# SyncE's DMAs in program order, with q's high parts first and three things traced later

## The chip, the cores and the metric

The kernel runs on one core of a Trainium2 chip. The metric is the device time of one execution in microseconds (us). TensorE (PE) multiplies, VectorE (DVE) and ScalarE (ACT) work on the results, GpSimd (POOL) helps, and SyncE (SP) issues nearly all DMAs; ACT issues the rest.

## What is computed

One layer of a streaming encoder, in float32, for a prompt of 2048 rows of 1024 and a sample of 32 rows. The reference, cut to what matters here:

```
mod = c @ w_mod + b_mod;  shift, scale, gate = split(mod, 3)
h = rms_norm(x, g_pre) * (1 + scale) + shift
z = h @ w_in      # a, b, z_conv, q, k, v, z_attn, g_conv, g_attn
u = a * sigmoid(b)
y_conv = (silu(layer_norm(conv31(u) + dw_b)) * silu(z_conv)) @ w_conv_out
o = attention(q, k, v)    # 8 heads of 64, own chunk of 64 rows and the 8 chunks before
y_attn = (o * silu(z_attn)) @ w_attn_out
merged = sigmoid(g_conv) * y_conv + sigmoid(g_attn) * y_attn
y = x + gate * rms_norm(merged @ w_o, g_post)
```

The prompt starts with no history. The sample attends to 512 cached rows of k and v besides its own. The last 512 rows of k and v (the cached ones moved on, for the sample) and the last 30 rows of u are outputs too.

## The kernel before

Every product is made in three passes: an operand is split into a high part (rounded, made by ACT) and a low part (the difference, made by DVE or POOL), and high*high, high*low and low*high are added in PSUM. So each projection of 128 columns is 24 matmuls per segment of rows.

The prompt goes in four batches of 512 rows; the sample's 32 rows ride with the first (batch 0, whose segments are 272 columns wide). Each batch has these stages: V's projection; attention, with the other projections of the batch ("fill", in the order that `FILL(b)` lists) traced between its pieces; the gate columns and the two branches; the output projection with the next batch's GLU columns; the norm and the residual. In `FILL`, a letter is a group of columns (`q`, `k`, `a` and `b` for u, `z` for the attention gate, `c` for the conv gate, `m` for a piece of the modulation) and the digit its block.

Weights come as `raw` tiles (512 KB, two buffers), are split into `w` (1 MB, three buffers) and, where they are used again, kept in DRAM (`kept`, written by ACT's queue) and later read back into `w`. `weights()` is called at the start of each projection and loads four entries of the plan ahead, splits two ahead. A load must wait until its buffer is free.

Heads go in pairs, `hp` from 0 to 3. In batch 0, `q_proj(hp)` loads the pair's cached rows of v and k into `zcb` (256 KB each) and starts `cached_k`, whose four transposes `pk` on PE turn the cached k. The bias of a head lies skewed in DRAM: `bias_write(h)` writes `bias_d[h]` from `lrow_d` (384 KB, DRAM to DRAM), then two small masks (`msk`) over it, and `load_bias(h)` reads it into `bias` (two buffers); in batch 0 `load_bias(h)` first traces `bias_write(h + 2)`. `sink_q` makes `qh` (ACT) and `ql` (DVE) from a projection. `turn` makes the high and low parts of transposed scores, `pth` and `ptl`. `turn_o` transposes the sample's attention output (`po`). `spill_v` writes the batch's V rows to `vs_d` for the next batch.

What sets the order: the program is traced once by hand-written generators with a pace model (`pace.start(gen, delay)` traces a piece when the modelled PE time has moved on by the delay, in us). For the engines named in `ENGINES`, PE, DVE, ACT and POOL, the instructions stand as traced. SP is not among them: a scheduler places its DMAs, as early as buffers allow and stores late. On SP an issue waits on SyncE itself, and what stands behind it waits too.

```
LEAD, LEADU, LEADU0 = 0.36, -3.0, -1.0
ENGINES = {mybir.EngineType.PE, mybir.EngineType.DVE, mybir.EngineType.Activation, mybir.EngineType.Pool}
...
            if b < NB - 1:
                pace.start(spill_v(b, vcur), 100.0 if b == 0 else 30.0)
...
    ctx.enter_context(tc.manual_schedule(engines=ENGINES))
```

Of the kernel before, what the change touches and what calls it, by code (L numbers as in the profile page):

```python
# [11 lines left out]
AF = mybir.ActivationFunctionType  # L12
# [35 lines left out]
TP = (1, 1, 1)  # L48

LEAD, LEADU, LEADU0 = 0.36, -3.0, -1.0  # L50
ENGINES = {mybir.EngineType.PE, mybir.EngineType.DVE, mybir.EngineType.Activation, mybir.EngineType.Pool}


def FILL(b):

    part = dict(q=C_Q, k=C_K, a=C_A, b=C_B, z=C_ZA, c=C_ZC, m=C_MOD)
    order = "b0 a0 q1 k1 b1 m0 a1 m1 b2 m2 q2 m3 k2 m4 a2 m5 z0 m6 b3 m7 a3 z1 q3 k3 z2 z3 c0 c1 c2 c3" if b == 0 else \
        "q1 k1 z0 q2 k2 z1 q3 k3 z2 z3 c0 c1 c2 c3"
    return [(int(x[1]), part[x[0]]) for x in order.split()]


def dram(ap, off, dims):
    return bass.AP(tensor=ap.tensor, offset=ap.offset + off, ap=[list(d) for d in dims])
# [77 lines left out]
def mixer_kernel(ctx, tc, x_prompt, x_sample, c_prompt, c_sample, cache_conv, cache_k, cache_v,  # L141
# [3 lines left out]
    act = nc.scalar.activation  # L145
    G = nc.gpsimd
    pace = Pace()
# [345 lines left out]
    conv_ready, ln_done, gate_done = set(), {}, set()  # L493
# [78 lines left out]
    def mod_part(i):  # L572


        n, kp = i // 4, i % 4
        m4, bm, gr = aof[0:4, 3, 0:512], aof[0:2, 2, 0:512], aof[0:2, 1, 0:512]
        if kp == 0:
            nc.sync.dma_start(bm, dram(b_mod, 2 * D + n * 512, [[0, 2], [1, 512]]))
            nc.sync.dma_start(gr, dram(g_post, n * 512, [[0, 2], [1, 512]]))
        wh, wl = weights(("mod", 2 * kp, (4 + n) * 512))  # L580
        pm = pp_tile("pm")
        for kk in range(2):
            mm(pm[0:4], c4[:, 2 * kp + kk, :], wh[:, kk, :], kk == 0, False)
            mm(pm[0:4], c4[:, 2 * kp + kk, :], wl[:, kk, :], False, kk == 1)
            yield
        if kp == 0:
            act(m4, pm[0:4], AF.Copy)
        else:
            V.tensor_tensor(m4, pm[0:4], m4, op=OP.add)
        if kp == 3:  # L590
            pace.start(gate_row(n, m4, bm, gr), 4.0)
# [17 lines left out]
    def spill_v(b, vcur):  # L609
        for t in range(4):  # L610
            nc.sync.dma_start(vs_d[b][:, t], vcur[:, t].bitcast(F32))
            yield 6.0
# [20 lines left out]
    with tc.tile_pool(name="init", bufs=1) as ini:  # L633
        mraw, mparts, m4 = {}, {}, {}
# [177 lines left out]
    for b in range(NB):  # L812
# [5 lines left out]
        with tc.tile_pool(name="at", bufs=1) as at:  # L818
# [26 lines left out]
                    o = (nvs[0, 0, 512 - TS:512] if t == 4 else nvp[0, 0, t * P:(t + 1) * P])  # L845
                    nc.sync.dma_start(o.rearrange("t h d -> t (h d)"), vo[0:m, 0:512])
            if b < NB - 1:
                pace.start(spill_v(b, vcur), 100.0 if b == 0 else 30.0)


            qls.clear()
# [25 lines left out]
            def q_proj(hp):  # L877
                while hp > 1 and ("s", hp - 2) not in ready:
                    yield "wait"
                qk_alloc(hp)  # L880
                kk, _, qh, ql = att[hp]
                ck = None
                if b == 0:
                    ck = zcb[:, 2 * (hp % 2), 0:512].rearrange("p (t c) -> p t c", c=P)
                    cv = cvs[hp] = zcb[:, 2 * (hp % 2) + 1, 0:512].rearrange("p (t c) -> p t c", c=P)
                    nc.sync.dma_start(cv, cache_v[0, 0].rearrange("t h d -> t (h d)")
                                      [:, hp * P:(hp + 1) * P].rearrange("(t p) c -> p t c", p=P))
                    nc.sync.dma_start(ck, cache_k[0, 0].rearrange("t h d -> t (h d)")
                                      [:, hp * P:(hp + 1) * P].rearrange("(t p) c -> p t c", p=P))

                    pace.start(cached_k(hp, ck), 9.9 if hp == 0 else 3.0)

                def sink_q(o, c0, c1):
                    for s in range(2):
                        r = slice(64 * s, 64 * s + 64)
                        act(qh[r, s, c0:c1], o[r], AF.Copy, scale=-0.125)
                        act(qh[64 - 64 * s:128 - 64 * s, s, c0:c1], o[r], AF.Copy, scale=-0.125)
                        V.scalar_tensor_tensor(ql[r, s, c0:c1], o[r], -0.125, qh[r, s, c0:c1].bitcast(F32),
                                               op0=OP.mult, op1=OP.subtract)

                yield from proj(C_Q + hp * P, b, sink_q)
# [127 lines left out]
            class Unit:  # L1029
# [77 lines left out]
                def turn(self, c):  # L1107

                    if c == 0:
                        self.ph = at.tile([P, PTW], F32R, tag="pth", name="pth", bufs=2)  # L1110
                        self.pl = at.tile([P, PTW], F32R, tag="ptl", name="ptl", bufs=2)
                    if c >= len(self.chunks):
                        return
                    pt = ps.tile([P, 512], F32, tag="T", name="pt", bufs=2)
                    if self.g == 2:
                        sp = self.sp[0]
                        for j in range(4):
                            transpose(pt[:, j * TS:(j + 1) * TS], sp[0:TS, j * P:(j + 1) * P], ident[0:TS, 0:TS])
                        transpose(pt[0:TS, 4 * TS:5 * TS], sp[0:TS, 512:512 + TS], ident[0:TS, 0:TS])
                        jobs = [(P, 0, 0, 4 * TS), (TS, 4 * TS, 4 * TS, 5 * TS)]  # L1120
                    else:
                        q, part = self.chunks[c]
                        for jj, (i, j) in enumerate(part):
                            transpose(pt[:, jj * P:(jj + 1) * P], self.sp[i][:, j:j + P], ident)
                        jobs = [(P, 0, q * P, (q + len(part)) * P)]
                    for r, o, f0, f1 in jobs:
                        act(self.ph[0:r, f0:f1], pt[0:r, o:o + f1 - f0], AF.Copy)  # L1127
                        V.tensor_tensor(self.pl[0:r, f0:f1], pt[0:r, o:o + f1 - f0],
                                        self.ph[0:r, f0:f1].bitcast(F32), op=OP.subtract)

                def mix(self):
                    hp, s, g, f, nk = self.hp, self.s, self.g, self.f, self.nk
                    if g == 2:

                        pv = ps.tile([P, 512], F32, tag="PV", name="pvs")
                        for j in range(5):
                            k = P if j < 4 else TS
                            rt = att[hp][1][:, j, s, :] if j < 4 else vsam[hp // 2][0:TS, 2 * (hp % 2) + s, :]
                            for w, ptx in enumerate((self.ph, self.pl)):
                                mm(pv[0:TS, 0:P], ptx[0:k, j * TS:(j + 1) * TS], rt, j == 0 and w == 0, j == 4 and w == 1)  # L1140
                        th = at.tile([TS, HD], F32, tag="osh", name="osh", bufs=2)
                        if s == 0:
                            osm[hp] = at.tile([TS, P], F32, tag="osm", name="osm", bufs=2)
                        act(th, pv[0:TS, 0:HD], AF.Copy)
                        V.tensor_tensor(osm[hp][:, s * HD:(s + 1) * HD], pv[0:TS, HD:P], th, op=OP.add)
                        if s == 1:
                            pace.start(turn_o(hp), 1.0)
                    else:
                        e = [2 * g + 5, 2 * g + 6]
                        common = list(range(f[1], e[0]))  # L1150
                        jobs = [(kt, 0, 2) for kt in common]
                        jobs += [(kt, 0, 1) for kt in range(f[0], common[0])]
                        jobs += [(kt, 1, 1) for kt in range(common[-1] + 1, e[1])]
                        if g == 0:
                            pvt[s] = ps.tile([P, 512], F32, tag="PV", name="pv")
                        c0 = g * 256
                        for j, (kt, i, n) in enumerate(jobs):
                            for w, ptx in enumerate((self.ph, self.pl)):
                                off = i * nk[0] + (kt - f[i]) * P
                                rhs = view(ptx, off, [[nk[0] + (f[0] - f[1]) * P, 2], [1, P]] if n == 2 else [[1, P]])  # L1160
                                mm(pvt[s][:, c0 + i * P:c0 + (i + n) * P], vtile(hp, s, kt), rhs,
                                   j == 0 and w == 0, j == len(jobs) - 1 and w == 1)
                        if g == 1:
                            put_o(hp, s, pvt[s], 0, TB)
                    if s == 1 and g == (2 if b == 0 else 1):
                        ready.add(("o", hp))
                        gates()
# [287 lines left out]
```

## Time and profile before

| what | before |
|---|---|
| median of three runs | 1741.46 us (1741.26 to 1746.23) |
| the profiled execution's own time | 1743.5 us |
| its span, from first to last instruction | 1741.4 us |
| PE busy | 1674.9 us (96%) |
| DVE, ACT, POOL busy | 65%, 37%, 12% |
| mean granted TensorE clock | 0.991 of 2.4 GHz |
| moved by DMA | 361.27 MB, 207 GB/s |

The span is what the trace shows; 2.1 us of the execution's own time lie outside it. An engine that waits is idle in the profile, and the view of waits says for whom. SP is never busy by the profile; its rows show when each DMA was issued.

### The profile page before, as it was taken

To read this page: it belongs to the slowest core of one execution; us is meant where nothing else is said; L and a number is where in the kernel's file an instruction comes from. 1 tells how busy PE (TensorE), PEld (TensorE's weight loads), DVE (VectorE), ACT (ScalarE), POOL (GpSimd) and SP (SyncE) were. 2 spreads that over 40 slices of the span, in tenths; PEclk is the share of its full clock that TensorE was granted. 3 is DMA by queue.
4 is the path that set the end of the run, shared out by engine and by line. 5 is a ranking of instruction groups with operands and counts; after the bars stand their busy time and mean duration, and the time that the engine had idled before them with its cause. 6 is when DMAs were issued, how large, how long until landed. Compare 5 with 4: busy or idle time off the path is not lost.

```text
span 1741.4 us, 23645 instructions
## 1 busy us (share of the span) xinstructions
PE 1674.9 (96%) x9221; PEld 1425.8 (82%) x9221; DVE 1135.9 (65%) x2055; ACT 646.5 (37%) x1232; POOL 210.3 (12%) x171
## 2 busy tenths in 40 slices
PE   6988889999999999999999999999999999999997
PEld 4877789899877788888888888888888888888886
DVE  6568778796818767676745967773544967665423
ACT  6645444325611255523430055531330045531211
POOL 0224433003200000000220000001130000001120
PEclk9999899999999999999999999999999999999999
DMA  9775555733666764477655674365555674355553
GB/s 288 223 279 201 189 204 200 277 110 119 225 241 217 289 254 162 160 261 266 218 209 190 247 275 172 132 229 189 194 205 193 223 251 163 135 189 190 189 194 145
DMA packets 144870, 361.27 MB, mean 207 GB/s; under 512 B 9326, under 2 KB 89386, under 8 KB 116311
## 3 DMA queue, kind: packets, MB, share of 16 engines
q1 hardware_dynamic: 136119, 296.85, 49.7%
q10 hardware_dynamic: 8640, 62.92, 8.8%
q8 instruction: 73, 1.20, 0.3%
q14 instruction: 38, 0.31, 0.0%
HBM read 273.07 MB, written 91.77 MB: 210 GB/s over the span
## 4 chain that ended last, share of the span: by engine, by line
PE 63%; DMA 2%; DVE 1%; ACT 0%; POOL 0%; issue 0%; POOLq 0%; DVEq 0%; ACTq 0%; SPq 0%
PE pj L155 35%; PE py L155 8%; PE pv L155 4%; PE sps L155 3%; PE pt L159 3%; PE op L155 3%; PE oT L155 2%; PE oS L155 2%; PE vS L155 1%; PE vT L155 1%; PE oP L155 1%; DMA w<-kept 1%; DMA kept<-w 0%; PE pxt L159 0%; DMA raw<-in_w_in_dram 0%; DVE pre L136 0%
## 5 line engine op out<-in xcount | busy, mean ns | idle before, releaser
L155 PE MATMUL pj<-hh,w 128*128 128x512 f32 (+1 forms) x4800 | 975.8, 357 | 14.0 <-DVE aof L136 4.0
L155 PEld LDWEIGHTS pj<-hh,w 128*128 128x128 f32 x4800 | 782.1, 190 | 136.3 <-issue 7.9
L136 DVE SCALAR_TENSOR_TENSOR y<-u,dww,y 128x512 f32<-128x512 f32 (+1 forms) x480 | 348.2, 785 | 0.5
L1092 ACT ACTIVATE sp<-sp,mn 128x640 f32<-128x640 f32 (+5 forms) x136 | 103.7, 762 | 132.0 <-DVE mn L136 132.0
L1127 ACT ACTIVATE pth<-pt 128x256 fp32r<-128x256 f32 (+4 forms) x184 | 91.8, 500 | 130.1 <-PE pt L159 118.0
L234 ACT ACTIVATE w<-raw 128x1024 fp32r<-128x1024 f32 x86 | 90.3, 1053 | 99.2 <-DMA raw<-in_w_in_dram 30.5
L136 DVE TENSOR_TENSOR ptl<-pt,pth 128x256 fp32r<-128x256 f32 (+4 forms) x184 | 104.1, 566 | 24.3 <-ACT pth L1127 23.0
L136 DVE CUSTOM_DVE_ANT_0 sp<-sps,bias 128x640 f32<-128x640 f32 (+4 forms) x128 | 94.1, 736 | 23.2 <-PE sps L155 22.2
L155 PE MATMUL py<-ah,w 128*128 128x512 f32 (+1 forms) x480 | 95.7, 355 | 7.8 <-DVE t L136 5.7
L236 POOL TENSOR_TENSOR w<-raw,w 128x1024 fp32r<-128x1024 f32 x32 | 81.3, 2547 | 150.7 <-ACT w L234 114.2
L155 PEld LDWEIGHTS py<-ah,w 128*128 128x128 f32 x480 | 79.5, 191 | 21.3 <-DVE t L136 6.1
L136 DVE TENSOR_TENSOR w<-raw,w 128x1024 fp32r<-128x1024 f32 x54 | 69.5, 1288 | 41.5 <-ACT w L234 40.9
L159 PE MATMUL pt<-ident,sp 128*128 128x128 f32 (+1 forms) x600 | 94.4, 273 | 0.0
L155 PE MATMUL py<-cohi,w 128*128 128x512 f32 (+1 forms) x320 | 90.1, 357 | 1.5 <-DVE mg L136 1.5
L540 POOL TENSOR_TENSOR u<-y 128x512 f32<-128x512 f32 (+1 forms) x4 | 5.3, 1325 | 646.7 <-DVE y L136 593.8
L136 DVE TENSOR_SCALAR sp<-sp,ll 128x640 f32<-128x640 f32 (+5 forms) x136 | 78.6, 578 | 4.8
L155 PE MATMUL sps<-kk,qh 128*128 128x320 f32 (+1 forms) x224 | 69.8, 319 | 8.7 <-DVE mn L136 6.2
L159 PEld LDWEIGHTS pt<-ident,sp 128*128 128x128 f32 (+1 forms) x600 | 69.1, 140 | 3.6 <-issue 1.5
L155 PE MATMUL sps<-kk,ql 128*128 128x320 f32 (+1 forms) x224 | 68.1, 311 | 0.0
L1319 ACT ACTIVATE t<-pj 128x512 f32<-128x512 f32 (+1 forms) x40 | 20.7, 516 | 127.2 <-PE pj L155 127.2
L1355 POOL TENSOR_TENSOR mg<-mg,t 128x512 f32<-128x512 f32 (+1 forms) x32 | 46.4, 1449 | 155.6 <-issue 102.2
L155 PEld LDWEIGHTS py<-cohi,w 128*128 128x128 f32 x320 | 56.7, 188 | 9.8 <-DVE mg L136 2.2
(254 smaller groups left out, 2207.3 us busy)
## 6 DMA issues: line engine op xcount, KB each, us to landing
w<-kept SPq DMA_DIRECT2D x162, 1024.0 KB
kept<-w ACTq DMA_DIRECT2D x60, 1024.0 KB
raw<-in_w_in_dram SPq DMA_DIRECT2D x62, 512.0 KB
bias<-bias_d SPq DMA_DIRECT2D x32, 320.0 KB
xt<-in_x_prompt_dram SPq DMA_DIRECT2D x16, 512.0 KB
wm<-in_w_mod_dram SPq DMA_DIRECT2D x16, 512.0 KB
xr<-in_x_prompt_dram SPq DMA_DIRECT2D x16, 512.0 KB
vs_d<-vcur SPq DMA_DIRECT2D x12, 512.0 KB
```

Source lines behind the costliest of these rows:

```text
L136: return fn(out, *a, **k)
L155: nc.tensor.matmul(out, lhsT=lhsT, rhs=rhs, start=start, stop=stop)
L159: nc.tensor.transpose(out, in_, idn)
L234: act(wh, raw, AF.Copy)
L236: (V if on_v else G).tensor_tensor(wl, raw, wh.bitcast(F32), op=OP.subtract)
L540: G.tensor_tensor(s2[:, 0:YW], Y[2][:, 0:YW], Y[3][:, 0:YW], op=OP.add)
L1092: self.ex[i] = lambda: act(sp[0:m, 0:nk], sp[0:m, 0:nk], AF.Exp, bias=mn[0:m], scale=-1.0, accum_out=ll[0:m])
L1127: act(self.ph[0:r, f0:f1], pt[0:r, o:o + f1 - f0], AF.Copy)
L1319: pace.run(proj(C_GC + m * P, b, lambda o, c0, c1: act(t1[:, c0:c1], o, AF.Tanh, scale=0.5)))
L1355: G.tensor_tensor(mg, mg, t2, op=OP.add)
```

## The change

Five edits. SP joins the engines whose instructions stand in the order of the trace. In `sink_q` all four high parts are traced ahead of the two low parts, and in `turn` the high parts of all jobs ahead of the low ones. In `FILL` for batch 0 block 3 of q and k comes ahead of block 1 of z. `turn_o` is traced 3.0 later than its unit in place of 1.0. V's rows of batches 1 and 2 are written 100 later in place of 30. An assertion is added too, which makes no instruction.

```
-ENGINES = {mybir.EngineType.PE, mybir.EngineType.DVE, mybir.EngineType.Activation, mybir.EngineType.Pool}
+ENGINES = {mybir.EngineType.PE, mybir.EngineType.DVE, mybir.EngineType.Activation, mybir.EngineType.Pool,
+           mybir.EngineType.SP}
...
-    order = "b0 a0 q1 k1 b1 m0 a1 m1 b2 m2 q2 m3 k2 m4 a2 m5 z0 m6 b3 m7 a3 z1 q3 k3 z2 z3 c0 c1 c2 c3" if b == 0 else \
+    order = "b0 a0 q1 k1 b1 m0 a1 m1 b2 m2 q2 m3 k2 m4 a2 m5 z0 m6 b3 m7 a3 q3 k3 z1 z2 z3 c0 c1 c2 c3" if b == 0 else \
...
-                pace.start(spill_v(b, vcur), 100.0 if b == 0 else 30.0)
+                pace.start(spill_v(b, vcur), 100.0)
...
-                    for s in range(2):
-                        r = slice(64 * s, 64 * s + 64)
+                    rows = [slice(0, 64), slice(64, 128)]
+                    for s, r in enumerate(rows):
                         act(qh[r, s, c0:c1], o[r], AF.Copy, scale=-0.125)
-                        act(qh[64 - 64 * s:128 - 64 * s, s, c0:c1], o[r], AF.Copy, scale=-0.125)
+                        act(qh[rows[1 - s], s, c0:c1], o[r], AF.Copy, scale=-0.125)
+                    for s, r in enumerate(rows):
                         V.scalar_tensor_tensor(ql[r, s, c0:c1], o[r], -0.125, qh[r, s, c0:c1].bitcast(F32),
                                                op0=OP.mult, op1=OP.subtract)
...
                     for r, o, f0, f1 in jobs:
                         act(self.ph[0:r, f0:f1], pt[0:r, o:o + f1 - f0], AF.Copy)
+                    for r, o, f0, f1 in jobs:
                         V.tensor_tensor(self.pl[0:r, f0:f1], pt[0:r, o:o + f1 - f0],
                                         self.ph[0:r, f0:f1].bitcast(F32), op=OP.subtract)
...
-                            pace.start(turn_o(hp), 1.0)
+                            pace.start(turn_o(hp), 3.0)
```

Where it moves instructions. First SP in batch 0, ahead of the first pair's attention. Before, the cached rows of the first two pairs (`zcb`) are issued around the write of `lrow_d`, ahead of the first bias writes:

```order
L641 DMA wm<-in_w_mod_dram 128x4x256 x2
L886 DMA zcb<-in_cache_v_dram 128x4x128
L777 DMA lrow_d<-aof 8x768
L888 DMA zcb<-in_cache_k_dram 128x4x128
L886 DMA zcb<-in_cache_v_dram 128x4x128
L888 DMA zcb<-in_cache_k_dram 128x4x128
L625 DMA bias_d_101<-lrow_d 128x768
```

In the change the first pair's stand after the sample's V rows (`vo`), a third head's bias write with its masks, and the first bias load:

```order
L225 DMA raw<-in_w_in_dram 128x8x128 x2
L848 DMA out_dram<-vo 32x512
L627 DMA bias_d_103<-lrow_d 128x768
L629 DMA bias_d_103<-msk 64x64
L630 DMA bias_d_103<-msk 64x64
L1021 DMA bias<-bias_d_101 128x640
L888 DMA zcb<-in_cache_v_dram 128x4x128
L890 DMA zcb<-in_cache_k_dram 128x4x128
```

The two loads of pair 0 moved behind six DMAs, two of which wait for another's landing or for ACT; those of pair 1 moved further down.

Second, SP at the third pair (`hp` 2). Before, its k rows were issued while pair 0's attention ran, with no bias write near:

```order
L1018 DMA bias<-bias_d_103 128x640
L886 DMA zcb<-in_cache_v_dram 128x4x128
L224 DMA raw<-in_w_in_dram 128x8x128
L888 DMA zcb<-in_cache_k_dram 128x4x128
L606 DMA out_dram<-in_cache_v_dram 16x15360
L224 DMA raw<-in_w_mod_dram 128x2x512
```

In the change the third pair's two loads stand here:

```order
L627 DMA bias_d_107<-lrow_d 128x768
L629 DMA bias_d_107<-msk 64x64
L630 DMA bias_d_107<-msk 64x64
L1021 DMA bias<-bias_d_105 128x640
L225 DMA raw<-in_w_mod_dram 128x2x512
L888 DMA zcb<-in_cache_v_dram 128x4x128
L890 DMA zcb<-in_cache_k_dram 128x4x128
```

The loads moved behind a bias write with its masks, a bias load, and the load of a piece of `w_mod` that waits for a free buffer.

Third, PE at the last pair of batch 0, after the sample's product with v (`pvs`). Before:

```order
L155 MATMUL pvs<-vsam,ptl 32x128
L155 MATMUL pj<-hh,w 128x272 x42
L159 MATMUL pu<-ident,u 30x128 x4
L155 MATMUL pj<-hh,w 128x272 x36
L159 MATMUL pk<-ident,zcb 128x128 x4
```

And in the change:

```order
L156 MATMUL pvs<-vsam,ptl 32x128
L156 MATMUL pj<-hh,w 128x272 x30
L160 MATMUL pk<-ident,zcb 128x128 x4
L156 MATMUL pj<-hh,w 128x272 x9
L160 MATMUL pu<-ident,u 30x128 x4
```

The last pair's transposes `pk` moved up by 48 matmuls and four transposes.

## Rows read from the trace of the kernel before

**Rows 1.** The page, part 1: busy us, share and instructions of each engine.

```profile
PE 1674.9 (96%) x9221; PEld 1425.8 (82%) x9221; DVE 1135.9 (65%) x2055; ACT 646.5 (37%) x1232; POOL 210.3 (12%) x171
```

**Rows 2.** Windows: busy us (instructions) of each engine by stretch, granted clock, DMA.

```profile
core 0: us, PE busy (x) PEld busy (x) DVE busy (x) ACT busy (x) POOL busy (x), PEclk, DMA share, GB/s
75.00:320.00 245.00, 218.26 (x1620) 198.65 (x1620) 181.69 (x389) 119.71 (x276) 83.30 (x36) 0.96 0.62 213
590.00:990.00 400.00, 396.91 (x1950) 330.55 (x1949) 271.91 (x469) 143.12 (x260) 32.45 (x34) 1.00 0.62 223
...
131.00:134.00 3.00, 3.00 (x16) 3.00 (x14) 2.94 (x7) 1.09 (x3) 0.73 (x1) 0.50 0.27 72
182.00:189.00 7.00, 6.37 (x21) 4.38 (x22) 3.50 (x6) 0.89 (x4) 0.00 (x0) 0.51 0.14 43
```

**Rows 3.** Waits: who waited for whom, us in total, times, longest.

```profile
PE po L159 <- DVE osm L136: 3.8, 4, 1.2
PE pj L155 <- DVE ql L136: 2.8, 3, 2.2
...
DVE ql L136 <- ACT qh L897: 29.6, 34, 1.8
```

**Rows 4.** Timeline of PE: start, us, instructions [idle before, releaser].

```profile
83.50 0.63 PE L159 MATMUL pk<-ident,zcb 128*128 128x128 f32 x4
...
94.83 0.45 PE L155 MATMUL sps<-kk,qh 128*128 128x384 f32 x1 [3.32 <-DVE mn L136]
...
108.77 0.60 PE L159 MATMUL pk<-ident,zcb 128*128 128x128 f32 x4
...
164.31 0.60 PE L159 MATMUL pk<-ident,zcb 128*128 128x128 f32 x4
...
182.63 1.86 PE L595 MATMUL pg<-aof,sel 4*2 4x512 f32 x2 [2.51 <-DVE ql L136]
...
247.29 4.77 PE L155 MATMUL pj<-hh,w 128*128 128x272 f32 x36
251.90 0.60 PE L159 MATMUL pk<-ident,zcb 128*128 128x128 f32 x4
...
613.51 1.87 PE L155 MATMUL pj<-hh,w 128*128 128x512 f32 x7 [2.57 <-DMA w<-kept]
...
1414.22 0.85 PE L155 MATMUL pj<-hh,w 128*128 128x512 f32 x3
```

**Rows 5.** Timeline of ACT, batch 0.

```profile
47.04 1.06 ACT L651 ACTIVATE wmh<-wm 128x1024 fp32r<-128x1024 f32 x1 [0.40 <-DMA wm<-in_w_mod_dram]
...
77.12 0.62 ACT L844 ACTIVATE vo<-vj 32x512 f32<-32x512 f32 x1
...
90.87 1.06 ACT L234 ACTIVATE w<-raw 128x1024 fp32r<-128x1024 f32 x1 [3.45 <-DMA raw<-in_w_in_dram]
```

**Rows 6.** Timeline of SP: issue of each DMA, us that issuing took.

```profile
59.24 0.50 SPq L625 DMA_DIRECT2D bias_d<-lrow_d  x1
...
60.47 0.52 SPq L1018 DMA_DIRECT2D bias<-bias_d  x1
63.98 0.46 SPq L627 DMA_DIRECT2D bias_d<-msk  x1
...
82.87 0.90 SPq L224 DMA_DIRECT2D raw<-in_w_in_dram  x1
...
102.65 0.37 SPq L224 DMA_DIRECT2D raw<-in_w_mod_dram  x1
...
163.41 0.37 SPq L224 DMA_DIRECT2D raw<-in_w_mod_dram  x1
...
242.59 0.26 SPq L599 DMA_DIRECT2D gp_d<-aof  x1
...
1408.05 0.33 SPq L846 DMA_DIRECT2D out_dram<-vo  x1
```

**Rows 7.** Chain that ended last: start, us, what.

```profile
604.54 8.84 DMA w<-kept
```

More of the change, by code (lines that the diff above doesn't have):

```diff
@@ L577, in mod_part @@
         if kp == 0:
+            assert len(gate_done) == n
             nc.sync.dma_start(bm, dram(b_mod, 2 * D + n * 512, [[0, 2], [1, 512]]))
```

## Prediction, made before the changed kernel ran

> **What bounds the kernel now.** I read the page's engine line first. TensorE is busy for 1674.9 of the 1741.4 us [rows 1], so 66.5 us of idle time or of modelled overlap is all that any reordering can recover, and a new wait of TensorE is nearly always a loss. Next I read the windows, to see where slack lies. From 590 to 990 us TensorE is busy for 396.9 of 400 us, at full clock. In batch 0's attention, from 75 to 320 us, it is busy for 218.3 of 245, so 26.7 us are idle, and the clock averages 0.96 [rows 2]. That is where four of the five edits act. The waits and TensorE's timeline then say what the idle time is: the four `po` transposes wait 3.8 us in total for VectorE's `osm`, projections wait 2.8 us for `ql` [rows 3], and single gaps of 3.32 us at 94.83, 2.51 at 182.63 and 2.57 at 613.51 stand out [rows 4]. The four `pk` transposes show no gap ahead of them: before the change the cached k is always there [rows 4].
>
> The sum is made in the span of the profiled execution. That execution took 1743.5 us, 2.1 outside its span, and the median of the runs is 1741.46, within 0.1 of the span. So I put the differences on 1741.5.
>
> **SP in program order: the loads of the cached k.** An SP issue waits on SyncE itself, and all that stands behind it waits too. In the changed order each pair's `zcb` loads stand behind a bias write, whose mask must wait until the write has landed. The trace shows that delay: `bias_d` is issued at 59.24, the mask over it at 63.98, 4.74 later [rows 6]. No row isolates the landing of a 256 KB load of `zcb`. The bounds are a quarter of what 1 MB took, 8.84/4 = 2.2 us [rows 7], and the 8.0 us of a 512 KB `raw` load issued at 82.87 in heavy traffic [rows 6], used at 90.87 [rows 5]. I take 4.0, nearest to the 4.74 of 384 KB just named.
>
> - Pair 0. The sample's `vo` is ready on ACT at 77.12 + 0.62 = 77.74 [rows 5]; its store goes (0.45), then the bias write; its mask 4.74 later, at about 82.9; then two masks, the bias load and the v half, four issues of about 0.5 [rows 6], so the k half is issued at 84.9 and lands at 88.9. TensorE wants it at 83.50 [rows 4]: **+5.4** (3.6 to 9.4).
> - What this gives back. The 3.32 us gap at 94.83 [rows 4] goes with ACT's wait of 3.45 us for the late `raw` at 90.87 [rows 5]. The other work that crowded that load has moved away in the new order, so I take that gap as gone: **-3.3**. Hence everything after runs 5.4 - 3.3 = 2.1 later.
> - Pair 1. The load stands behind the `w_mod` piece of 102.65 [rows 6], so 102.65 + 2.1 + 0.4, then 4.74 for the write, 2.0 for the four issues and 4.0 to land: 115.9. TensorE wants it at 108.77 + 2.1 = 110.9: **+5.0**.
> - Pair 2. Here the gate is the `w_mod` piece at 163.41 + 0.37 [rows 6], which waits for a buffer. With the v half (0.5) ahead, 164.3 + 4.0 = 168.3 against 164.31 [rows 4]: **+4.0**.
> - Pair 3. The gate is the store of `gp_d`, 242.59 + 0.26 + 0.5, and 4.0 to land: 247.35. The `FILL` edit moves `pk` up by 48 matmuls, at 4.77/36 us each [rows 4], 6.4 us, and by four transposes (0.35): 251.90 - 6.7 = 245.2. **+2.1**.
>
> All four carry the same 4.0. At 2.2 each is 1.8 less, at 8.0 each is 4.0 more. A rule of the Trainium skill ("DMA: Bandwidth & Descriptors", section "Anatomy of one DMA — SWDGE (gpsimd) path") speaks against the change: DMA engines do not wait on semaphores, any such wait happens on the issuing sequencer, ahead of dispatch. Its fit of 2.0 us plus the bytes at 436 GB/s would give, as an estimate, 2.6 us for 256 KB, and the sum would come out 4 x 1.4 = 5.6 us lower. The trace's 8.0 us for 512 KB does not agree with that fit under traffic.
>
> **The clock after a stall.** Two stretches show it at half: 0.50 from 131 to 134, and 0.51 from 182 to 189, right after the 2.51 us gap [rows 2, 4]. The second cost 7.0 x 0.49 = 3.4 us. For the three stalls of 4 us and more I take between 0 and 3.4 each, 1.5: **+4.5** (0 to 10).
>
> **SP elsewhere.** At the start two of the `wm` loads now stand behind a load of `raw` that waits for a buffer; ACT already waits 0.40 for the last `wm` at 47.04 [rows 5]: **+1** (0 to 4). At the start of batch 3 a weight load for the next q now stands behind all four `vo` stores, the last of which waits for ACT and went at 1408.05 [rows 6]. Behind it, the bias and kk loads, it goes at about 1409.4 and lands 4.0 to 8.84 later [rows 7], at 1413.4 to 1418.2 against TensorE's 1414.22 [rows 4]: **+2** (0 to 4). Against that, the 2.57 us gap at 613.51 is a `w<-kept` late [rows 4] because its transfer, 8.84 us from 604.54 [rows 7], shared the engines with loads of k and v that the scheduler had hoisted; in the new order they stand later: **-2.6** (0 to -2.6). The copies of the old caches to the outputs, the loads of x and the gate rows and the V stores that move later stand nowhere in front of a waiting engine that I can find: zero. Their cover is that nothing in the kernel reads the outputs and that the V rows are read a batch later; where that cover fails, a late V block would show as a wait at the next batch's `vh`.
>
> **High parts first.** VectorE waits 34 times for ACT's `qh`, 29.6 us in total [rows 3]. ACT's own order is unchanged; only its wait for VectorE between two halves goes. Most of it is off TensorE's path. What TensorE pays is the 2.8 us of waits of the projections and the 2.51 at 182.63 [rows 3, 4], 5.3 in all; with the second low part still behind the same ACT work I take **-3** (0 to -5.3).
>
> **`turn_o` later.** In the changed order `po` stands some 24 matmuls further down, 24 x 4.77/36 = 3.2 us [rows 4], more than the longest wait of 1.2 [rows 3]. The waits go, but for what the last pair may keep: **-3.2** (of 3.8).
>
> Sum: stalls 5.4 - 3.3 + 5.0 + 4.0 + 2.1 = 13.2; clock +4.5; start and batch 3 +3; gains -2.6 - 3 - 3.2 = -8.8. Together +11.9, so 1741.5 + 11.9 = about **1753 us**.
>
> **The rivals.** *Cancelled:* the cached k lands in 2.2 us, the clock never falls, and the start and batch 3 cost their 3. Stalls 13.2 - 7.2 = 6.0, +3, -8.8: 1741.7 us. For it speaks that 256 KB is little; against it that the row in traffic is 8.0.
>
> *Faster, because the stalls are given back:* while TensorE waits for `pk`, ACT and VectorE work off what TensorE would have waited for later. In the 26.7 us of idle time [rows 2], beyond the 3.3, 2.5 and 3.8 already taken, 17 us are left that a lead of the other engines can absorb. If all 13.2 and the clock's 4.5 are absorbed, what remains is 3 - 8.8 = -5.8: 1735.7 us. It decides the sign from 11.9 us of give-back on. Against it: a gap is given back only where another engine's lateness made it, and the one at 94.83, which I count already, is the only long one right behind a stall.
>
> *Slower still, one long queue:* the loads take 8.0 us as `raw` did, and each stall ends at half clock for 3.4. Stalls +16, clock 13.6 in place of 4.5: 11.9 + 25.1 = 37, 1778 us.
>
> **How the numbers follow.** I give the forecast 0.55, cancelled 0.20, faster 0.17, slower still 0.08. The forecast's own range is 1747 to 1764: landings of 3 and clock 2 at the low end (-4, -2.5), landings of 5.5 and clock 9.5 at the high end (+6, +5). Eight in ten asks for all of that, the cancelled case with its spread (1737 to 1747), and the upper half of the faster case: 1735 to 1767. Some 0.3%, 5.2 us, is what a measurement tells from no change. By that, faster has 0.18, the same 0.20, slower 0.62.
>
> **What would show it.** In the profile after, TensorE waits for a DMA `zcb<-in_cache_k` at `pk` near 83, 111, 170 and 255, and SP shows `vo`, `bias_d`, masks, `bias`, `zcb` in a row with the gap of some 4.7 us ahead of the first mask. Half clock follows the first three. The gap at 94.83 is gone, as are the `po` waits and the one near 613; `ql` waits are shorter; TensorE may wait for `w<-kept` near 1414. The prediction is wrong if `pk` starts without a wait, which would mean that the masks don't hold SP or that the loads go early enough, or if the stalls are there and the span of 75 to 320 is no longer all the same.

## The result, and the profile after

The change makes the kernel slower: 1786.51 us (1785.5 to 1789.06) against 1741.99, a ratio of 1.0254 with an interval of 1.0241 to 1.0266. The direction was forecast; the size, 44.5 us against some 12, lies far outside the range of 1747 to 1764, and beyond the slowest rival, 1778.

The page of the changed kernel, part 1, answers to [rows 1]:

```profile
PE 1690.3 (95%) x9221; PEld 1438.9 (81%) x9221; DVE 1134.4 (63%) x2055; ACT 645.6 (36%) x1232; POOL 210.9 (12%) x171
```

The span is 1787.1 us, 45.7 longer. TensorE does the same 9221 matmuls, but is busy for 15.4 us more: that is the clock. By the clock records of the two traces it is busy at half clock for 22.0 us before and for 57.0 us after; half of these 35.0 us is 17.5, enough for the 15.4. It is idle or overlapped for 1787.1 - 1690.3 = 96.8 us in place of 66.5, 30.3 more: those are stalls. So a third of the loss is the clock; the prediction had 4.5 us for it. The waits of TensorE in the changed kernel (us in total, times, longest) name the stalls, beside [rows 3]:

```profile
PE pk L160 <- DMA zcb<-in_cache_k_dram: 23.7, 4, 7.3
PE vS L156 <- DMA w<-kept: 9.0, 2, 4.9
PE pj L156 <- DVE aof L137: 6.9, 4, 3.5
PE pj L156 <- DMA w<-kept: 5.5, 2, 5.3
PE pg L597 <- DVE ql L137: 2.8, 1, 2.8
PE pj L156 <- ACT t L1324: 2.6, 1, 2.6
PE pj L156 <- DVE ql L137: 2.2, 2, 2.0
...
PE po L160 <- DVE osm L137: 0.5, 1, 0.5
```

Both kernels issue almost the same row of matmuls, so the place of a loss is best read by counting them: the start of the n-th matmul in one trace less its start in the other. Worked out so from the two traces (us):

```
n      before   after   lag    what stands there
241      56.0    58.8    2.7   start of the kernel
481      96.8   104.7    7.9   behind pk of pair 0 and what is given back
561     107.5   114.7    7.2
681     124.9   137.8   12.8   behind pk of pair 1
1161    205.9   223.8   17.9   behind pk of pair 2
1801    299.9   324.9   25.0   behind pk of pair 3 and the waits for aof
2201    355.5   375.0   19.5
2601    405.7   430.4   24.7   behind the wait for ACT's t
5401    956.9   979.9   23.0   batches 0 and 1 done
5801   1040.8  1071.2   30.4   start of batch 2
7401   1365.1  1395.4   30.4
7521   1393.0  1430.2   37.3   start of batch 3
7641   1418.8  1464.4   45.6   first q of batch 3
9221   1731.4  1777.1   45.7   last
```

More than half of the loss, 25.0 us, is made by 300 us; 22.6 (7.4, 6.9 and 8.3) come at three places at the starts of batches 2 and 3, and some 2 are given back between. SP's timeline and TensorE's show both. First SP ahead of pair 0 (start, us for the issue):

```profile
80.49 0.34 SPq L848 DMA_DIRECT2D out_dram<-vo  x1
80.88 0.51 SPq L627 DMA_DIRECT2D bias_d<-lrow_d  x1
85.32 0.46 SPq L629 DMA_DIRECT2D bias_d<-msk  x1
85.84 1.06 SPq L630 DMA_DIRECT2D bias_d<-msk  x1
86.95 0.71 SPq L1021 DMA_DIRECT2D bias<-bias_d  x1
87.70 0.43 SPq L888 DMA_DIRECT2D zcb<-in_cache_v_dram  x1
88.18 0.51 SPq L890 DMA_DIRECT2D zcb<-in_cache_k_dram  x1
```

The forecast queue stands there, hold at the mask and all; the k half is issued at 88.18, and TensorE's `pk` starts at 93.51, 5.3 us later (the start and the idle time ahead, with who ended it):

```profile
93.51 1.09 PE L160 MATMUL pk<-ident,zcb 128*128 128x128 f32 x4 [7.33 <-DMA zcb<-in_cache_k_dram]
...
1018.70 2.93 PE L156 MATMUL vS<-w,hh 128*128 128x512 f32 x6 [4.93 <-DMA w<-kept]
...
1424.11 2.50 PE L156 MATMUL vS<-w,hh 128*128 128x512 f32 x5 [4.10 <-DMA w<-kept]
...
1454.28 3.32 PE L156 MATMUL pj<-hh,w 128*128 128x512 f32 x7 [5.26 <-DMA w<-kept]
```

And SP at the start of batch 2, in the changed kernel:

```profile
997.08 0.32 SPq L239 DMA_DIRECT2D w<-kept  x1
1007.57 4.13 SPq L1408 DMA_DIRECT2D out_dram<-pre  x4
1011.80 15.28 SPq L239 DMA_DIRECT2D w<-kept  x4
```

The four stores of the finished rows (`pre`) wait for VectorE until 1007.57; the next load of V's weights stands behind them and goes at 1011.80. In the kernel before, the same load was issued at 979.70, ahead of the stores at 984.59 (these are the loads with the same number in the two kernels, counted as the matmuls were):

```profile
979.70 0.32 SPq L238 DMA_DIRECT2D w<-kept  x1
984.59 3.98 SPq L1404 DMA_DIRECT2D out_dram<-pre  x4
```

At the start of batch 3 the same happens once more behind `pre` (1378.57 before, 1417.85 after), and then behind `vo`. There the load that TensorE waits for at 1454.28 stands behind all four stores; in the kernel before it went at 1400.78, ahead of the first of them. SP in the changed kernel:

```profile
1438.74 5.83 SPq L848 DMA_DIRECT2D out_dram<-vo  x4
...
1445.72 1.02 SPq L239 DMA_DIRECT2D w<-kept  x2
```

The clock behind such stalls, by windows of the changed kernel, each beginning near the end of its stall:

```profile
92.00:98.00 6.00, 4.49 (x20) 4.52 (x21) 1.85 (x4) 2.46 (x5) 0.00 (x0) 0.50 0.64 196
...
1018.00:1026.00 8.00, 7.30 (x22) 5.81 (x23) 4.93 (x8) 0.00 (x0) 0.00 (x0) 0.66 0.47 200
1423.00:1431.00 8.00, 6.89 (x19) 5.47 (x20) 6.18 (x10) 0.00 (x0) 0.00 (x0) 0.58 0.61 259
1453.00:1461.00 8.00, 6.72 (x22) 5.65 (x22) 0.83 (x2) 0.58 (x1) 0.00 (x0) 0.57 0.93 370
```

### The profile page after: what moved, and what is told of

Same layout as the page of the kernel before. It is cut to its first block, busy times and chain, and to the rows that moved or that the text cites. A ratio compares the mean times of both kernels' runs of the same rounds, so it can differ in the third digit from the quotient of the medians.

```text
span 1787.1 us, 23658 instructions
## 1 busy us (share of the span) xinstructions
PE 1690.3 (95%) x9221; PEld 1438.9 (81%) x9221; DVE 1134.4 (63%) x2055; ACT 645.6 (36%) x1232; POOL 210.9 (12%) x171
## 4 chain that ended last, share of the span: by engine, by line
PE 56%; DVE 4%; DMA 3%; ACT 2%; issue 1%; SPq 0%; DVEq 0%; ACTq 0%
PE pj L156 31%; PE py L156 7%; PE pv L156 3%; PE sps L156 3%; PE op L156 3%; PE pt L160 2%; PE oT L156 2%; PE oS L156 2%; DVE pre L137 1%; DMA w<-kept 1%; DVE sp L137 1%; PE oP L156 1%; PE vS L156 1%; ACT sp L1095 1%; DMA bias<-bias_d 1%; PE vT L156 1%
## 5 line engine op out<-in xcount | busy, mean ns | idle before, releaser
L1323 ACT ACTIVATE t<-pj 128x512 f32<-128x512 f32 (+1 forms) x40 | 20.6, 516 | 128.8 <-PE pj L156 128.8
```

What stands on the lines that cost most here:

```text
L1323: pace.run(proj(C_GC + m * P, b, lambda o, c0, c1: act(t1[:, c0:c1], o, AF.Tanh, scale=0.5)))
```

## The experiments

**One part alone, and all but one.** Two kernels split the change. The first (other4_alone) leaves SP to the scheduler and keeps the four other edits, the second (sp_alone) is the kernel before with SP added to `ENGINES` and nothing else:

```
+           mybir.EngineType.SP}
```

> The change without SP among the ordered engines: the four other edits alone. Theory (all of the loss comes from SP's program order): no wait of TensorE for the cached k at pk, none for w<-kept at the starts of batches 2 and 3, and the small gains of the other edits remain, 3.2 for po and up to 3 for ql: 1733 to 1741 us. Rival (the other edits, above all q3 and k3 ahead of z1, bring a good part of the loss, since waits on aof of 1.8 and 3.5 us stand near 231 and 235 in the changed kernel): 1747 us or more, with those waits in place.

> The kernel before with SP added to the ordered engines and nothing else. Theory: the whole loss and none of the small gains, 1786 to 1794 us, with four waits at pk of 23 us or more in total. Rival (other edits bring part of it): below 1780 us.

The four edits alone took 1742.4 us, a ratio of 1.0006 (0.9995 to 1.0018): no difference. SP alone took 1788.11, ratio 1.0266 (1.025 to 1.0281), with 25.3 us of waits at `pk`. So the whole loss is SP's order, and the rival for the other edits falls. The gain that I expected of the four edits, some 3 to 6 us, is missed. In the one execution that was traced the lag is -4.0 at 205.9 us and 0.0 again at 405.7, behind a wait for ACT's `t` (a gate) that the kernel before does not have. What the -4.0 is worth comes out further down. The wait, in TensorE's timeline of other4_alone:

```profile
402.47 2.81 PE L155 MATMUL pj<-hh,w 128*128 128x272 f32 x12 [2.63 <-ACT t L1323]
```

**The cached k early.** In cache_hoisted the `zcb` loads of the changed kernel are traced earlier, by a function `cached(hp)` that holds them (the edit, cut):

```
+                    cached(0)
+                    cached(1)
                     bias_write(0)
...
                                       [:, hp * P:(hp + 1) * P], ko[0:m, 0:P])
+                    cached(hp + 2)
```

> The changed kernel, in which only the loads of the cached k and v are traced earlier: pairs 0 and 1 ahead of the first bias write, pair hp+2 behind the store of the new k rows of pair hp. Theory: the four waits at pk go (23.7 us of waiting; the lag behind the kernel before grows by 8.9, 7.7, 8.3 and 3.6 us around them and 8 of it is given back right behind), so some 20 us are won: 1763 to 1770 us. Rival (the stalls only make room for other late loads in the same crowded stretch, so raw or the bias comes late in their place): above 1777 us, with new waits of DVE or ACT for raw or bias between 75 and 300 us.

It took 1763.63 us, ratio 1.0112 (1.0089 to 1.0134), 22.9 below the changed kernel. No wait for `zcb` is left. The lag at 299.9 is -3.1 in place of 25.0 in the traced execution, whose 1755.96 us is 7.7 below the median of the four; both_repaired below, in which every engine has the same order up to there, has 5.4. So the measure is the medians: 22.9 us of the loss are shown to be the place of eight loads.

**The weights a step early.** In w_ahead three loads of the changed kernel are traced ahead of the stores that held them (the edit, cut):

```
             if b < NB - 1:
+                if b:
+                    w_parts(used[0] + 2)
                 store(0, 5 if b == 0 else 4, 1)
...
+            if b == NB - 1:
+                w_parts(used[0] + 2)
             for t, q0, m in tok_tiles(b):
```

> The changed kernel, in which only three weight loads are traced one step earlier: the third load of V's weights ahead of the output stores at the end of batches 1 and 2, and a load for the next q ahead of the stores of vo in batch 3. Theory (these loads stand behind stores that wait on SP, and TensorE waits for them at the starts of batches 2 and 3: the lag grows by 7.4, 6.9 and 8.3 us there, stall and half clock together): the waits for w<-kept at 1018.7, 1424.1 and 1454.3 go, 1763 to 1770 us. Rival (the loads are late because their buffer comes free late, not because of the store ahead of them): 1782 to 1787 us, the waits in place.

It took 1767.39, ratio 1.0144 (1.0127 to 1.0161), 19.1 below. SP's timeline at the start of batch 2 now has five weight loads in a row, then the stores:

```profile
976.10 22.71 SPq L239 DMA_DIRECT2D w<-kept  x5
1003.38 3.92 SPq L1410 DMA_DIRECT2D out_dram<-pre  x4
```

The three waits are gone, and 0.5 us of waits for `w<-kept` is left in all; the lag goes from 18.8 at 956.9 only to 19.3 at the end. The rival (the buffer) falls.

**Both.** The two edits together are both_repaired.

> The changed kernel with the cached rows loaded early and the three weight loads a step earlier, both at once. Theory (two separate places on SP, nothing shared): the two gains add up, 1786.5 - 22.9 - 19.1 = 1744.5, so 1742 to 1748 us, no wait of TensorE for zcb or for w<-kept. Rival (one repair uncovers the other's wait, or the earlier loads crowd others): 1750 us or more.

1742.91 us, ratio 0.9998 (0.9988 to 1.0007): the two gains, 22.9 and 19.1, make 42.0 us, and together the edits win 43.6. That is the whole loss.

**What makes the cached k late.** The prediction had put it on the hold at the mask, 4.74 us, and a landing of 4.0. Three kernels take that apart, each with the loads where the change has them. The first, masks_later, traces the masks one `load_bias` later (the edit, cut):

```
                 if b == 0:
+                    bias_mask(h + 1)
                     bias_write(h + 2)
```

> The changed kernel, in which only the two masks over a head's bias are traced one load_bias later than its bias write, so that SP no longer waits there for a write that was just issued; the loads of the cached k stand where they stood. Theory (the 3.9 to 5 us for which a mask holds SP are the greater part of the stalls at pk of pairs 0 to 2, and pair 3 has another gate): the waits at pk fall from 23.7 to about 11 us, pair 3's 3.4 unchanged; 1774 to 1780 us. Rival (the stores and w_mod loads ahead, or the landing itself beside 384 KB of bias write, set the time): the waits stay above 18 us and the time above 1782 us.

My theory fell. 1781.77 us, ratio 1.0221 (1.0205 to 1.0237), and the waits at `pk` are 23.7 us as in the change, though SP is no longer held, as its timeline in masks_later shows:

```profile
80.58 0.59 SPq L627 DMA_DIRECT2D bias_d<-lrow_d  x1
81.27 0.53 SPq L1027 DMA_DIRECT2D bias<-bias_d  x1
81.85 0.43 SPq L893 DMA_DIRECT2D zcb<-in_cache_v_dram  x1
82.33 0.51 SPq L895 DMA_DIRECT2D zcb<-in_cache_k_dram  x1
```

TensorE's timeline of the same kernel, at `pk` of pair 0:

```profile
91.27 1.09 PE L160 MATMUL pk<-ident,zcb 128*128 128x128 f32 x4 [6.53 <-DMA zcb<-in_cache_k_dram]
```

The k half goes 5.9 us earlier and lands in 8.9 us in place of 5.3. What the mask no longer holds, the bytes ahead do; the second kernel shows it. The time is 4.7 us below the change all the same, between the two that were expected. The waits at `pk` have no part in that; of the others, the longest for `aof` falls from 3.5 to 2.3 us, and the rest is not traced to a cause.

The second kernel, no_later_bias_writes, leaves the bias writes of heads 2 to 7 and their masks out (the edit, cut):

```
-        if h < H:
+        if h < 2:
             nc.sync.dma_start(dram(bias_d[h], 0,
...
-                    nc.sync.dma_start(bias[h], dram(bias_d[h], 127,
+                    nc.sync.dma_start(bias[h], dram(bias_d[h % 2], 127,
```

> The changed kernel without the bias writes and masks of heads 2 to 7 (every head reads the bias of head 0 or 1, so the attention is not the reference's); all else, the place of the zcb loads too, as in the change. Theory (SP's order costs the stalls of pairs 0 to 2 by the bias write ahead: first by the hold at the mask, and without the hold by the bytes of the 384 KB DRAM-to-DRAM write in the same queue): the waits at pk of pairs 0, 1 and 2 fall from 20.3 to under 7 us in total, pair 3 keeps its 3.4; 1762 to 1770 us. Rival (the gates ahead, vo and w_mod, and the raw loads make it late anyway): the three waits stay above 14 us, 1778 us or more.

1764.53 us, ratio 1.012 (1.0106 to 1.0134). Pairs 0 and 1 start without a wait (at 85.26 the first, 4.2 us after the issue of its k half at 81.09). Pair 2 keeps 5.0 us: its loads stand on SP behind a `raw` of `w_mod` that waits for a buffer, the gate that the prediction named; `pk` starts at 165.17, 5.1 us after the issue of the k half. SP's timeline there:

```profile
159.14 0.37 SPq L225 DMA_DIRECT2D raw<-in_w_mod_dram  x1
159.56 0.46 SPq L888 DMA_DIRECT2D zcb<-in_cache_v_dram  x1
160.08 0.50 SPq L890 DMA_DIRECT2D zcb<-in_cache_k_dram  x1
```

Pair 3 also lost its wait for `zcb`, which I had not expected; `pk` waits 2.7 us for VectorE's `ql` in its place. The third kernel, zcb_on_ACT_queue, keeps the writes and issues the eight loads on ACT (`nc.scalar` in place of `nc.sync`):

> The changed kernel with the eight zcb loads issued by ACT in place of SP, at the same place of the trace; on ACT the first pair stands right behind the copy of vo. Theory (what makes the load late is its place on SP behind the bias write): it is issued before or beside the bias write, lands in some 5 us, and the four waits fall from 23.7 to under 8 us; 1764 to 1771 us. Rival (the load shares the 16 engines with bias write, bias and raw whoever issues it, and ACT is no earlier there): the waits stay above 15 us, 1777 us or more.

1771.6 us, ratio 1.0159 (1.0146 to 1.0173), waits for `zcb` 5.2 us in two. The k half of pair 0 goes 1.2 us ahead of the bias write and `pk` has no wait. ACT's issues in this kernel:

```profile
79.89 0.44 ACTq L888 DMA_DIRECT2D zcb<-in_cache_v_dram  x1
...
80.38 0.52 ACTq L890 DMA_DIRECT2D zcb<-in_cache_k_dram  x1
```

And SP's bias write beside them:

```profile
81.59 0.51 SPq L627 DMA_DIRECT2D bias_d<-lrow_d  x1
```

The gain is 14.9 us, and the time stands just above the expected 1764 to 1771. Lesser waits of 2.5 and 2.7 us stay at pairs 1 and 2: ACT issues those k halves at 109.91 and 164.48, only 2.4 and 3.3 us before TensorE wants them.

**Whether the other edits win anything.** Two kernels, SP left to the scheduler. The first, other4_without_turn_o, has the four edits but for this one:

```
-                            pace.start(turn_o(hp), 3.0)
+                            pace.start(turn_o(hp), 1.0)
```

> The four other edits alone, with turn_o back at 1.0, SP left to the scheduler. Theory (the later turn_o shifts the paced pieces of the conv's norm, so that on ACT a gate's t stands behind u, which waits for VectorE's 2.9 us of y, and TensorE loses 4.9 us near 400 us with half clock; this eats what the edits win before): the wait of 2.6 us for ACT's t near 402 goes, the po waits of some 3 us come back, 1737 to 1741 us. Rival (the loss near 400 us comes from another edit or from the earlier arrival of the work): the wait stays, 1741 to 1745 us.

The second, other4_norm_later, has all four, and the conv norm of batch 0 traced later:

```
-        yield YL[1]
+        yield YL[1] + (0.5 if b == 0 else 0.0)
```

> The four other edits alone, with turn_o at 3.0 and batch 0's conv norm traced 0.5 later after its first split, so that ACT again has t ahead of u as in the kernel before; SP left to the scheduler. Theory: po waits and the wait near 402 us are both gone, 1734 to 1739 us, faster than before. Rival (what is gained ahead of 400 us is given back to another late engine anyway): 1741 to 1744 us.

1744.32 (ratio 1.0006, 0.9997 to 1.0015) and 1741.15 (0.9992, 0.9982 to 1.0002). In both the projections' wait for `t` near 402 is gone, so the later `turn_o`, through the pace, does move it there; in the first the `po` waits are back, 4.3 us in four. But neither is measurably faster. In the second TensorE waits instead 1.3 us for VectorE's `y` near 407, and 2.2 for VectorE's `t` near 446, where other4_alone waited 1.6.

The times are those of the rival, but its reason, that a gain ahead of 400 us is given back, is not shown. Up to there other4_alone and other4_norm_later have the same order on every engine, and yet the lag at 205.9 is -4.0 in the one traced execution and 0.2 in the other. Most of this arises from 176 to 196 us: `pg` waits 1.67 us in the first and 2.77 in the second, and from 184 to 192 us the granted clock is 1.00 in the first and 0.58 in the second. So the -4.0 belongs to that execution and its clock, and whether the four edits win anything stays open.

**A version that beats both.** The changed kernel with all three repairs (all_three_repaired), and with the later norm as well (all_three_norm_later):

> The changed kernel with the cached rows loaded early, the three weight loads a step earlier and the masks one load_bias later. Theory (in both_repaired 7.0 us are still lost near 212 to 219 us, where ACT waits 6 us for a raw that stood behind a mask on SP, and VectorE and TensorE behind it; with the masks later that raw goes 2 to 3 us earlier): the wait of 3.5 us for aof near 219 shrinks to 1.6 or less and half clock goes with it, 1735 to 1740 us. Rival (the raw is late by its buffer or its landing, as the cached k was in masks_later): 1741 to 1745 us, the wait in place.

> The same with batch 0's conv norm traced 0.5 later, so that ACT has t ahead of u. Theory: another 2 to 4 us, 1732 to 1738 us. Rival (other4_norm_later gained nothing measurable; VectorE is late there whatever ACT's order): as all_three_repaired within 1.5 us.

1740.04 us, ratio 0.9979 (0.997 to 0.9988), and 1739.95, ratio 0.9978 (0.9967 to 0.9989). Both are faster than the kernel before, by some 0.2%, with intervals clear of 1, but less than the 0.3% that the prediction held to be the least that can be told; the first was expected at 1735 to 1740. The later norm adds nothing that can be measured, as its rival said. The masks' move helps here, where it did not at `pk`: ACT's wait for a `raw` that stood behind a mask falls from 5.75 to 1.53 us, and TensorE's wait for `aof` behind it from 3.52 to 2.32. First the rows of ACT and of TensorE in both_repaired:

```profile
210.24 1.06 ACT L235 ACTIVATE w<-raw 128x1024 fp32r<-128x1024 f32 x1 [5.75 <-DMA raw<-in_w_in_dram]
...
219.16 1.73 PE L156 MATMUL pj<-hh,w 128*128 128x272 f32 x6 [3.52 <-DVE aof L137]
```

And the same two in all_three_repaired:

```profile
204.82 1.06 ACT L235 ACTIVATE w<-raw 128x1024 fp32r<-128x1024 f32 x1 [1.53 <-DMA raw<-in_w_in_dram]
...
214.67 1.45 PE L156 MATMUL pj<-hh,w 128*128 128x272 f32 x6 [2.32 <-DVE aof L137]
```

## Why the prediction was right in sign and wrong in size

The sign came by the mechanism that was forecast, not by luck: SP's order alone brings the whole loss, and the place of the eight `zcb` loads half of it. The span grew by 45.7 us where the sum had 11.9, so 33.8 us are to be explained. 20.6 of them arise at the starts of batches 2 and 3 (22.6 against +2), and 12.5 by 300 us (25.0 against 13.2 + 4.5 + 1 - 3 - 3.2 = 12.5); some 2 are given back between, where the sum had 2.6.

- **The cached k: right mechanism, too small.** All four stalls came at the forecast places: 7.3, 6.7, 6.4 and 3.4 us, 23.7 in place of 16.5. From the issue of the k half to `pk` it took 5.3, 3.8, 5.9 and 5.8 us, not 4.0. Between the loads of pair 0 and those of pair 1 SP issues two bias writes, at 101.99 and 111.16; the sum had one. And the hold at the mask is not a price of its own: masks_later and no_later_bias_writes together show that without the hold the wait stays as long as the bytes of the bias write stand ahead of the load. Hold and bytes are one cost, not two terms.
- **The clock: mis-sized.** +4.5 was taken for three stalls; 15.4 us are measured over the kernel, in which half clock follows the weight stalls of batches 2 and 3 too. I took 1.5 a stall where [rows 2] showed 3.4 behind a gap of 2.5 us; the row at hand was the better price.
- **SP elsewhere: the step that failed.** The prediction says that stores and loads other than those named "stand nowhere in front of a waiting engine that I can find: zero". The stores of the finished rows were not in that list at all. At the starts of batches 2 and 3 they stand ahead of V's weights and cost 4.9 and 4.1 us of stall, 7.4 and 6.9 us of lag with the clock. The term for `vo` in batch 3 named the right mechanism, but priced +2 for what became 5.3 us of stall and 8.3 of lag: the load took 8.6 us from its issue at 1445.72, and the matmul that waits for it starts at 1411.57 in the kernel before, 2.65 us ahead of the 1414.22 that was taken. w_ahead gives 19.1 us back for these three.
- **The start** cost 2.7 us, not 1. In the traces of the other kernels with SP's order the lag there is 1.2 to 4.7 us, in the three with the scheduler's it is -0.5 to 0.2, so it is SP's order too.
- **Given back:** the 3.3 us gap at 94.83 is gone as forecast. The 2.57 at 613.51 is gone too; by the same count 1.6 us are won there and 1.8 lost again by 647 us of the kernel before.
- **High parts first** was to bring 3 us. The waits for `ql` are 2.8 + 2.2 = 5.0 us against 5.3: nothing. **`turn_o` later** took the `po` waits for `osm` from 3.8 to 0.5, as forecast, but moved a piece of the norm on ACT. From the four edits together no gain is measured.

## What to carry to other kernels

When a queue's order goes over from a scheduler to the program, look at every store that waits for a result, and ask which load stands behind it: here the ends of batches 1 and 2 had one, and the V projection of batch 3. A load belongs ahead of the big transfers whose bytes it would follow, not just ahead of their waits. And a stall of TensorE of some microseconds is priced with the half clock behind it, here about half as much again (15.4 us on 30.3).

## What was not expected of the hardware

Pair 0's k half, a load of 256 KB, took 8.9 us when it was issued right behind a 384 KB write from DRAM to DRAM and a 320 KB read (masks_later), at most 4.2 us without the write (no_later_bias_writes), and on another queue, 1.2 us ahead of the write, it was in time (zcb_on_ACT_queue). Other traffic counts too: without the write, but behind a 512 KB `raw`, pair 2's took 5.1 us. The estimate by the fit of the Trainium skill ("DMA: Bandwidth & Descriptors", section "Anatomy of one DMA — SWDGE (gpsimd) path"), 2.6 us, which the page gives for DMAs on GpSimd's path and not for SyncE's, is below the time of every k half whose landing ended a wait of `pk` (3.8 to 8.9 us). In batch 2 a stall of 4.9 us came with a granted clock of 0.66 over the 8 us from just before its end, and it cost 7.4 us in all. And one trace does not tell a gain of 4 us: with the same instructions in the same order, the gap at `pg` was 1.67 us with full clock behind it in one execution (other4_alone), and 2.77 us with a granted clock of 0.58 behind it in another (other4_norm_later).
